# Moving the rotation of head 0's queries and keys behind sums of the second and third value group, on VectorE alone

## The chip, the cores and the metric

The kernel runs on one core of a Trainium2 chip. Its time is the device time of one execution in microseconds (us). A group of runs is given by its median. The engines are named as the profile names them: PE is TensorE (matmuls), PEld its weight loads, DVE is VectorE, ACT is ScalarE, POOL is GpSimd and SP is SyncE, which here only issues transfers.

## What is computed

The reference is a two-layer encoder in float32 over 512 tokens of width 1024. Layer 0 mixes tokens with a bidirectional mLSTM, layer 1 with attention in three dilation groups; after each mixer come a SwiGLU and a gated embedding. The change touches only the beginning of layer 1's mixer. There the normed input is projected to queries, keys and values of 8 heads for each of 3 groups, and a quarter of every query and key is rotated by position:

```python
def apply_partial_rope(x, cos, sin):
    half = ROPE_DIM // 2
    x1 = x[..., :half]
    x2 = x[..., half:ROPE_DIM]
    rot = jnp.concatenate([x1 * cos - x2 * sin, x2 * cos + x1 * sin], axis=-1).astype(x.dtype)
    return jnp.concatenate([rot, x[..., ROPE_DIM:]], axis=-1)
...
    proj = (xn @ w_in).reshape(B, S, N_GROUPS, 3, A_HEADS, A_HEAD_DIM)
    for g, (window, dil) in enumerate(DILATED_GROUPS):
        q = apply_partial_rope(proj[:, :, g, 0], cos, sin)
        k = apply_partial_rope(proj[:, :, g, 1], cos, sin)
        o_g, l_g = dilated_window_attention(q, k, proj[:, :, g, 2], dil, window // 2 // dil)
```

## The kernel before

Every large product is made of three float32r matmuls (L124 to L126): each operand is split into a rounded high part and the rest. Weights come from HBM into a ring of four staging tiles (`wst`); ACT rounds a piece to `wh` (L116), DVE subtracts to `wl` (L117), each in a ring of three; PE then multiplies.

Each engine runs its own queue strictly in order. The order in a queue is made when the program is built: a scheduler picks among what the code traces, and `tc.issue_after(ins)` ties whatever is traced inside it, on the engine of `ins`, to a place behind `ins`.

Layer 1's mixer begins like this:

- Six products make the queries and keys of head 0 for the three groups. They are made ahead, before the norm's factors are known, and ACT copies them out of PSUM into the tiles `ahead` (L1074).
- `value_cell(g)` makes the values of all heads for group g. It uses a seven-product scheme in place of eight quarter products: a11, s1, s2, s4, s3, a12, a22, in this order, each on quarters of the weights. One product is 2 halves (one `wh`/`wl` pair each) of 12 matmuls, so a group is 7 x 24 = 168 matmuls. Two of the seven weight operands are sums of two quarters, which POOL's queue makes by a second, accumulating transfer onto a landed quarter (L809); two others are made in place by DVE (L835, L838). Between the products DVE adds and subtracts the results (L850, L854, and the sums of outputs c12 at L859, c22 at L865, c21 at L875), and ACT evicts c11 (L870) and scales and stores the others (L831).
- `value_cell(0)` runs first. Then `qk_head(0, ahead)` rotates the six tiles of head 0, then `value_cell(1)` and `value_cell(2)` follow in the code, then `scores`.
- A rotation, `rope_evict`, is four instructions: DVE multiplies the tile by the cosines (L881) and shuffles 32 partitions (L883), POOL multiplies these by the sines (L884) and adds them in (L886). Group 0's query is then split into two parts by ACT and DVE (L951, L952); group 0's key is split into pieces by six copies on ACT (L941) and six subtractions on POOL (L942), with small fills (L944, L945). Where the tiles of group 0 are read, their tokens are reordered on the way, so operands are strided.

PSUM has three tiles of the kind `pj`, three of the kind `s` and two of the kind `o`. A value group takes three `pj`, one `s` and two `o`; its first and sixth product (a11, a12) use two `pj` tiles, which c11's eviction (L870) sets free for the next group.

Of the kernel before, what the change touches and what calls it, by code (L numbers as in the profile page):

```python
# [15 lines left out]
ALU = mybir.AluOpType  # L16
# [20 lines left out]
def encoder_kernel(  # L37
# [25 lines left out]
    V, A, G, T = nc.vector, nc.scalar, nc.gpsimd, nc.tensor  # L63
# [35 lines left out]
    def tok_a(t):  # L99
        return t.rearrange("p (u r) -> p u r", r=4)  # L100
# [48 lines left out]
    for hf in range(2):  # L149
        for i in range(4):  # L150
            if 4 * hf + i == 2:
                nc.sync.dma_start(nrow, norm_mix.rearrange("l (k p) -> (l k) p", p=P))
            t = ut()
# [130 lines left out]
    for hf in range(2):  # L284
        for i in range(4):
            t = ut()
# [398 lines left out]
    RS = cst.tile([32, S], F32, name="RS")  # L685
# [107 lines left out]

    vd = [dr.tile([S, D], F32, tag="vd", name=nm("vd"), bufs=3) for _ in range(3)]

    def value_cell(g):
        c0 = col(g, 2, 0)

        rows = vd[g].rearrange("(u r) c -> r u c", r=4) if g == 0 else vd[g].rearrange("(r u) c -> r u c", u=P)

        def part(e, c):
            return b_in[512 * e:512 * e + 512, c0 + 512 * c:c0 + 512 * c + 512].rearrange("(k p) c -> p k c", p=P)

        def quarter(e, c, plus=None):

            t = wp.tile([P, 4, 512], F32, tag="wst", name=nm("wst"), bufs=WST)
            nc.sync.dma_start(t, part(e, c))
            if plus:
                nc.gpsimd.dma_start(t, part(*plus), accum_op=ALU.add)  # L809
            return t  # L810

        def quad_product(o, name, w, prep=None, first=True):
            for e in range(2):
                d = w[:, 2 * e:2 * e + 2]
                if prep:
                    prep(d, slice(2 * e, 2 * e + 2))
                wh, wl = wsplit(d, (P, 2, 512))
                for t in range(2):
                    for kk in range(2):
                        xh, xl = n.quad(name, 2 * e + kk, t)  # L820
                        st = first and e == 0 and kk == 0
                        T.matmul(o[t], xh, wh[:, kk], start=st, stop=False, skip_group_check=True)
                        T.matmul(o[t], xh, wl[:, kk], start=False, stop=False, skip_group_check=True)  # L823
                        T.matmul(o[t], xl, wh[:, kk], start=False, stop=e == 1 and kk == 1,  # L824
                                 skip_group_check=True)

        def two():
            return [ut() for _ in range(2)]

        def store(t, half, c, src):  # L830
            A.activation(src, src, AF.Copy, scale=n.ra(2 * half + t))  # L831
            nc.sync.dma_start(rows[2 * half + t][:, 512 * c:512 * c + 512], src)

        def plus(b):
            return lambda d, ks: V.tensor_tensor(d, d, b[:, ks], op=ALU.add)  # L835

        def neg_plus(b):
            return lambda d, ks: V.scalar_tensor_tensor(d, d, -1.0, b[:, ks], op0=ALU.mult, op1=ALU.subtract)  # L838

        x_, z_, y_ = [ps(), ps()], [ps(), ps("s", (P, S), 3)], [ps("o", (P, S), 2) for _ in range(2)]  # L840
        b11, t1 = quarter(0, 0), quarter(0, 1, (0, 0))
        quad_product(x_, "a11", b11)
        m1 = two()
        for t in range(2):
            A.copy(m1[t], x_[t])
        b22 = quarter(1, 1)
        quad_product(z_, "s1", t1)
        w_ = two()
        for t in range(2):
            V.tensor_tensor(w_[t], z_[t], m1[t], op=ALU.subtract)  # L850
        quad_product(y_, "s2", t1, plus(b22))
        u2 = two()
        for t in range(2):
            V.tensor_tensor(u2[t], y_[t], m1[t], op=ALU.subtract)  # L854
        t3 = quarter(1, 1, (0, 1))
        quad_product(z_, "s4", b22, first=False)
        c12 = two()
        for t in range(2):
            V.tensor_tensor(c12[t], z_[t], u2[t], op=ALU.add)  # L859
            store(t, 0, 1, c12[t])  # L860
        b21 = quarter(1, 0)
        quad_product(y_, "s3", t3, first=False)
        c22 = two()
        for t in range(2):
            V.tensor_tensor(c22[t], y_[t], w_[t], op=ALU.add)  # L865
            store(t, 1, 1, c22[t])
        quad_product(x_, "a12", b21, first=False)
        c11 = two()
        for t in range(2):
            A.activation(c11[t], x_[t], AF.Copy, scale=n.ra(t))  # L870
            nc.sync.dma_start(rows[t][:, 0:512], c11[t])
        quad_product(y_, "a22", t1, neg_plus(b21), first=False)
        c21 = two()
        for t in range(2):
            V.tensor_tensor(c21[t], m1[t], y_[t], op=ALU.subtract)  # L875
            store(t, 1, 0, c21[t])

    def rope_evict(o, dst, b_layout):

        to = (lambda t: t) if b_layout else (lambda t: t.rearrange("p (r u) -> p u r", r=4))  # L880
        V.tensor_tensor(dst if b_layout else tok_a(dst), to(o), to(RC), op=ALU.mult)  # L881
        sh = ut((32, S))
        V.stream_shuffle(sh, o[0:32], [(e + 16) % 32 for e in range(32)])  # L883
        G.tensor_tensor(sh, sh, RS, op=ALU.mult)  # L884
        d = dst[0:32]
        G.tensor_tensor(d if b_layout else tok_a(d), d if b_layout else tok_a(d), to(sh), op=ALU.add)  # L886

    def values(pr):

# [20 lines left out]
    def product(g, s, h):  # L910

        c0 = col(g, s, h)
        stg = wp.tile([P, KT, 256], F32, tag="wst", name=nm("wst"), bufs=WST)
        nc.sync.dma_start(stg[:, :, :P], b_in[:, c0:c0 + P].rearrange("(k p) c -> p k c", p=P))
        wh, wl = wcols(stg, KT, 0)
        o = ps()
        for k in range(KT):
            mm3(o, wh[:, k], wl[:, k], n.xh[k], n.xl[k], k == 0, k == KT - 1)
        return o

    def qk_head(h, ahead=None):

        res = {}
        if ahead is None:
            ahead = {}
        for g in range(3):
            for s in range(2):
                o = ahead[g, s] if (g, s) in ahead else product(g, s, h)
                if g == 0 and s == 1:

                    t = ut()
                    rope_evict(o, t, False)
                    t4 = t.rearrange("p (i t) -> p i t", i=4)
                    kh, kl = ([ut((P, 2, 256), F32R) for _ in range(2)] for _ in range(2))

# [10 lines left out]
                    t = (kh, kl)  # L946
                elif g == 0:
                    t = ut()
                    rope_evict(o, t, False)
                    hi, lo = ut(dt=F32R), ut(dt=F32R)  # L950
                    A.copy(hi, t)  # L951
                    V.tensor_tensor(lo, t, f(hi), op=ALU.subtract)  # L952
                    t = (hi, lo)
                else:
                    t = ut()
                    rope_evict(o, t, True)
                res[g, s] = t
        return res

    def scores(qk):  # L960
        pA = [ut((P, 2, 256)) for _ in range(2)]
# [122 lines left out]
    V.tensor_tensor(RC[0:32], RC[0:32], rB[0:32], op=ALU.mult)  # L1084
    A.copy(RC[32:64], rB[32:64])
    A.copy(RC[64:P], rB[64:P])
    qk = qk_head(0, ahead)
    for g in range(1, 3):
        value_cell(g)
    probs = scores(qk)  # L1090
    for h in range(NH):
        if h % 2 == 0:
# [142 lines left out]
```

## Time and profile before

| | |
|---|---|
| Runs: median (lowest to highest of 3) | 1648.16 us (1646.62 to 1650.27) |
| The profiled execution's own time | 1647.76 us |
| Its span in the profile | 1646.1 us |
| DVE busy | 888.8 us (54%) |
| ACT busy | 629.1 us (38%) |
| POOL busy | 380.8 us (23%) |
| Transfers | 173.64 MB, 105 GB/s over the span |

A time in a row is counted from the start of the span. A row of the timeline gives the start, the duration, the engine, the line and the tiles, and in brackets how long the engine stood idle before it and what ended that. Matmuls overlap: with 512 columns one starts every 0.23 us, though each is shown longer. In a row of windows the columns are the length, each engine's busy time with the number of instructions, the granted TensorE clock as a share of full speed, the busy share of the DMA engines and GB/s. The three value groups lie between 731 and 866 us.

### The profile page before, as it was taken

Reading aid. Unit: us, or ns where it says so; the run is one execution under the profiler, and the core shown is the slowest. Engines: PE = TensorE matmul, PEld = TensorE weight load, DVE = VectorE, ACT = ScalarE, POOL = GpSimd, SP = SyncE. Lnnn points to the kernel's source line nnn. Section 1 sums busy time; section 2 is a strip of 40 time slices with the busy share of each in tenths; the row PEclk is TensorE's granted clock in tenths of the full one; section 3 lists DMA queues with packets and bytes.
Section 4 is the critical chain, followed back from the end, with each engine's and each line's share of the span. In section 5 each row is a group of like instructions: output and inputs, shape, how many; then the busy total and the mean of one; then the engine's idle time right before and its main releaser. Section 6 shows DMA issues by size and latency. Waiting matters only on the chain.

```text
span 1646.1 us, 20328 instructions
## 1 busy us (share of the span) xinstructions
PE 1601.9 (97%) x7892; PEld 1349.5 (82%) x7892; DVE 888.8 (54%) x1451; ACT 629.1 (38%) x1051; POOL 380.8 (23%) x459
## 2 busy tenths in 40 slices
PE   7899999999999999999899999999999999999998
PEld 6788998888888888787678788888788888888886
DVE  6755654444445333766867566666554444433353
ACT  5666543333232323654444233333343233223242
POOL 3455403000000010111604665656130000001000
PEclk9999999999999999999899999999999999999999
DMA  7322223223233322367466242425223323232221
GB/s 208 104 78 77 66 90 104 92 88 94 86 103 103 108 72 70 99 177 222 133 194 166 77 122 74 122 76 163 78 77 102 95 86 96 85 126 96 83 77 51
DMA packets 192496, 173.64 MB, mean 105 GB/s; under 512 B 16440, under 2 KB 171632, under 8 KB 192400
## 3 DMA queue, kind: packets, MB, share of 16 engines
q1 hardware_dynamic: 188096, 165.85, 32.7%
q0 software_dynamic: 3200, 6.36, 2.2%
q8 instruction: 62, 1.02, 0.3%
q10 hardware_dynamic: 1104, 0.13, 0.1%
q14 instruction: 34, 0.28, 0.1%
HBM read 163.85 MB, written 8.47 MB: 105 GB/s over the span
## 4 chain that ended last, share of the span: by engine, by line
PE 85%; DVE 3%; DMA 3%; POOL 2%; ACT 2%; issue 1%; POOLq 0%; SPq 0%; DVEq 0%; ACTq 0%
PE pj L124 19%; PE pj L125 19%; PE pj L126 19%; PE o L124 5%; PE o L126 5%; PE o L125 5%; PE o L498 2%; PE o L1031 2%; DMA wst<-in_b_w_in_dram 2%; DVE wl L117 1%; PE s L977 1%; ACT wh L116 1%; PE o L823 1%; PE o L824 1%; DMA swd<-st 1%
## 5 line engine op out<-in xcount | busy, mean ns | idle before, releaser
L116 ACT CAST wh<-wst 128x1024 fp32r<-128x1024 f32 (+2 forms) x285 | 289.5, 1020 | 653.7 <-PE pj L125 382.1
L124 PE MATMUL pj<-u,wh 128*128 128x512 f32 x1325 | 518.7, 391 | 2.7 <-ACT wh L116 1.5
L126 PE MATMUL pj<-u,wl 128*128 128x512 f32 x1325 | 517.6, 391 | 2.6 <-DVE wl L117 2.6
L125 PE MATMUL pj<-u,wh 128*128 128x512 f32 x1325 | 518.2, 391 | 0.0
L117 DVE TENSOR_TENSOR wl<-wst,wh 128x1024 fp32r<-128x1024 f32 (+3 forms) x283 | 341.6, 1208 | 212.8 <-ACT wh L116 212.4
L126 PEld LDWEIGHTS pj<-u,wl 128*128 128x128 f32 x1325 | 249.4, 188 | 55.5 <-DVE wl L117 4.4
L124 PEld LDWEIGHTS pj<-u,wh 128*128 128x128 f32 x1325 | 249.6, 188 | 54.8 <-ACT wh L116 2.2
L125 PEld LDWEIGHTS pj<-u,wh 128*128 128x128 f32 x1325 | 249.4, 188 | 50.5 <-DVE u L183 0.2
L241 POOL TENSOR_TENSOR u<-u,u 128x512 f32<-128x512 f32 x30 | 49.5, 1650 | 821.2 <-ACT u L237 820.9
L124 PE MATMUL o<-u,wh 128*128 128x512 f32 x375 | 146.1, 390 | 0.0
L126 PE MATMUL o<-u,wl 128*128 128x512 f32 x375 | 145.9, 389 | 0.0
L125 PE MATMUL o<-u,wh 128*128 128x512 f32 x375 | 145.9, 389 | 0.0
L884 POOL TENSOR_TENSOR u<-u,RS 32x512 f32<-32x512 f32 x48 | 90.4, 1883 | 127.7 <-DVE u L883 98.8
L613 DVE TENSOR_TENSOR u<-o,u 128x512 f32<-128x512 f32 x44 | 30.4, 691 | 127.5 <-PE o L126 123.7
L886 POOL TENSOR_TENSOR u<-u,u 32x512 f32<-32x512 f32 x48 | 82.3, 1715 | 3.8
L124 PE MATMUL pj<-wh,u 128*128 128x256 f32 (+1 forms) x272 | 79.3, 293 | 3.6 <-ACT u L432 3.6
L125 PEld LDWEIGHTS o<-u,wh 128*128 128x128 f32 x375 | 70.4, 188 | 14.6
L126 PEld LDWEIGHTS o<-u,wl 128*128 128x128 f32 x375 | 70.4, 188 | 14.6
L124 PEld LDWEIGHTS o<-u,wh 128*128 128x128 f32 x375 | 70.4, 188 | 14.5
L125 PE MATMUL pj<-wl,u 128*128 128x256 f32 (+1 forms) x272 | 79.5, 292 | 0.0
L126 PE MATMUL pj<-wh,u 128*128 128x256 f32 (+1 forms) x272 | 79.5, 292 | 0.0
L600 DVE TENSOR_TENSOR u<-pj,u 128x512 f32<-128x512 f32 x42 | 29.0, 691 | 81.9 <-PE pj L126 81.9
(316 smaller groups left out, 2056.1 us busy)
## 6 DMA issues: line engine op xcount, KB each, us to landing
wst<-in_b_w_in_dram SPq DMA_DIRECT2D x48, 512.0 KB, 3.8
wst<-in_w_gate_dram SPq DMA_DIRECT2D x22, 1024.0 KB, 5.3
wst<-in_w_up_dram SPq DMA_DIRECT2D x22, 1024.0 KB, 5.3
wst<-in_w_down_dram SPq DMA_DIRECT2D x16, 1024.0 KB, 5.2
wst<-in_b_w_in_dram SPq DMA_DIRECT2D x15, 1024.0 KB, 6.2
wst<-in_a_w_in_dram SPq DMA_DIRECT2D x8, 1024.0 KB, 5.3
wst<-in_ple_gate_dram SPq DMA_DIRECT2D x8, 1024.0 KB, 5.4
wst<-in_w_down_dram SPq DMA_DIRECT2D x8, 768.0 KB, 4.6
```

The source lines that it names most:

```text
L116: A.copy(hi, src)
L117: eng.tensor_tensor(lo, src, f(hi), op=ALU.subtract)
L124: T.matmul(o, ah, bh, start=start, stop=False)
L125: T.matmul(o, ah, bl, start=False, stop=False)
L126: T.matmul(o, al, bh, start=False, stop=stop_)
L241: (G if k < KT - 1 else V).tensor_tensor(self.q, self.q, s, op=ALU.add)
L498: T.matmul(o[:, d, :], pt[d][s][:, j * P:(j + 1) * P], vt[s][:, hh, :], start=s == ks[0], stop=s == ks[-1])
L600: V.tensor_tensor(gt, og_, n.rB, op=ALU.mult)
L613: V.tensor_tensor(u, ou, n.rB, op=ALU.mult)
L884: G.tensor_tensor(sh, sh, RS, op=ALU.mult)
L886: G.tensor_tensor(d if b_layout else tok_a(d), d if b_layout else tok_a(d), to(sh), op=ALU.add)
L1031: T.matmul(a_tile(o, i) if bi < 2 else b_tile(o, i), vv[i][:, e * P:(e + 1) * P], pt[:, i * P:(i + 1) * P], start=bi == 0 and i == 0, stop ...
```

## The change

`qk_head`'s body becomes a generator, `qk_steps`, that stops after each of the six query and key tiles. For head 0 the six steps are no longer traced between the first and the second value group: `value_cell(1)` and `value_cell(2)` each call one step behind the second half of c12, of c22 and of c21, inside `tc.issue_after` of that DVE instruction. So the order is query and key of group 0 and the query of group 1 in the second value group, then the key of group 1 and both of group 2 in the third. In these steps the two instructions that POOL did are done by DVE (`eng`); for heads 1 to 7 POOL keeps them.

```diff
@@ -793,7 +793,13 @@
-    def value_cell(g):
+    def value_cell(g, step=None):
+
+        def behind(ins):
+            if step:
+                with tc.issue_after(ins.ins):
+                    step()
+
...
@@ -856,14 +862,16 @@
         for t in range(2):
-            V.tensor_tensor(c12[t], z_[t], u2[t], op=ALU.add)
+            last = V.tensor_tensor(c12[t], z_[t], u2[t], op=ALU.add)
             store(t, 0, 1, c12[t])
+        behind(last)
         b21 = quarter(1, 0)
         quad_product(y_, "s3", t3, first=False)
         c22 = two()
         for t in range(2):
-            V.tensor_tensor(c22[t], y_[t], w_[t], op=ALU.add)
+            last = V.tensor_tensor(c22[t], y_[t], w_[t], op=ALU.add)
             store(t, 1, 1, c22[t])
+        behind(last)
...
         for t in range(2):
-            V.tensor_tensor(c21[t], m1[t], y_[t], op=ALU.subtract)
+            last = V.tensor_tensor(c21[t], m1[t], y_[t], op=ALU.subtract)
             store(t, 1, 0, c21[t])
-
-    def rope_evict(o, dst, b_layout):
+        behind(last)
+
+    def rope_evict(o, dst, b_layout, eng):
...
         V.stream_shuffle(sh, o[0:32], [(e + 16) % 32 for e in range(32)])
-        G.tensor_tensor(sh, sh, RS, op=ALU.mult)
+        eng.tensor_tensor(sh, sh, RS, op=ALU.mult)
         d = dst[0:32]
-        G.tensor_tensor(d if b_layout else tok_a(d), d if b_layout else tok_a(d), to(sh), op=ALU.add)
+        eng.tensor_tensor(d if b_layout else tok_a(d), d if b_layout else tok_a(d), to(sh), op=ALU.add)
...
-    def qk_head(h, ahead=None):
-
+    def qk_head(h):
         res = {}
-        if ahead is None:
-            ahead = {}
+        for _ in qk_steps(h, res):
+            pass
+        return res
+
+    def qk_steps(h, res, ahead=None):
+
+        eng = V if ahead else G
         for g in range(3):
             for s in range(2):
-                o = ahead[g, s] if (g, s) in ahead else product(g, s, h)
+                o = ahead[g, s] if ahead else product(g, s, h)
...
                 res[g, s] = t
-        return res
+                yield
...
-    qk = qk_head(0, ahead)
+    qk = {}
+    steps = qk_steps(0, qk, ahead)
     for g in range(1, 3):
-        value_cell(g)
+        value_cell(g, lambda: next(steps))
     probs = scores(qk)
```

In the changed kernel the lines that the text speaks of have other numbers: the rotation's four instructions L881, L883, L884, L886 are L890, L892, L893, L895 (all four on DVE for head 0); the in-place sums L835 and L838 are L841 and L844; L865, L870, L875, L941 are L872, L878, L883, L954; L850 and L859 are L856 and L865.

Three places in the queues matter below. Numbers in the names are buffers; `u_5854` and `u_5887` hold group 0's query and key of head 0.

DVE at the start of the second value group, before (first c21 of the first group, then rotations between the second group's weight pieces):

```order
L875 TENSOR_TENSOR u_6378<-u_6141,o_6102 128x512
L875 TENSOR_TENSOR u_6379<-u_6142,o_6103 128x512
L881 TENSOR_TENSOR u_6390<-u_5854,RC 128x512
L883 STREAM_SHUFFLE u_6392<-u_5854 32x512
L117 TENSOR_TENSOR wl_6500<-wst_6458,wh_6499 128x1024
L835 TENSOR_TENSOR wst_6458<-wst_6458,wst_6497 128x1024
L117 TENSOR_TENSOR wl_6516<-wst_6458,wh_6515 128x1024
L952 TENSOR_TENSOR u_6397<-u_6390,u_6396 128x512
L881 TENSOR_TENSOR u_6400<-u_5887,RC 128x512
L883 STREAM_SHUFFLE u_6402<-u_5887 32x512
L117 TENSOR_TENSOR wl_6537<-wst_6458,wh_6536 128x1024
```

DVE late in the second value group, now (from c12's second half to c22's second half; `wst_6566` and `wst_6398` are the weights of a12 and a22):

```order
L865 TENSOR_TENSOR u_6549<-s_6393,u_6510 128x512
L890 TENSOR_TENSOR u_6556<-u_5854,RC 128x512
L892 STREAM_SHUFFLE u_6558<-u_5854 32x512
L117 TENSOR_TENSOR wl_6635<-wst_6566,wh_6634 128x1024
L893 TENSOR_TENSOR u_6558<-u_6558,RS 32x512
L117 TENSOR_TENSOR wl_6651<-wst_6566,wh_6650 128x1024
L895 TENSOR_TENSOR u_6556<-u_6556,u_6558 32x512
L117 TENSOR_TENSOR wl_6674<-wst_6398,wh_6673 128x1024
L965 TENSOR_TENSOR u_6563<-u_6556,u_6562 128x512
L872 TENSOR_TENSOR u_6600<-o_6394,u_6471 128x512
L872 TENSOR_TENSOR u_6601<-o_6395,u_6472 128x512
```

The first rotation has moved from the start of the second group to behind c12, interleaved with the weight pieces of a12 and a22, and its last two steps have come over from POOL. The key's rotation follows in the same pattern behind c22, interleaved with a22's last piece and the third group's first.

DVE around the second group's third to fifth product (s2, s4, s3), before (`wst_6616` is the quarter b21, `wst_6497` and `wst_6573` the weights of s4 and s3):

```order
L117 TENSOR_TENSOR wl_6577<-wst_6497,wh_6576 128x1024
L854 TENSOR_TENSOR u_6569<-o_6454,u_6493 128x512
L854 TENSOR_TENSOR u_6570<-o_6455,u_6494 128x512
L117 TENSOR_TENSOR wl_6593<-wst_6497,wh_6592 128x1024
L117 TENSOR_TENSOR wl_6619<-wst_6573,wh_6618 128x1024
L838 SCALAR_TENSOR_TENSOR wst_6458<-wst_6458,wst_6616 128x1024
L859 TENSOR_TENSOR u_6608<-pj_6452,u_6569 128x512
```

DVE at the second group's third product (s2, pieces `wl_6477` and `wl_6494`), now (`wst_6566` is b21, `wst_6437` the weights of s4):

```order
L117 TENSOR_TENSOR wl_6477<-wst_6398,wh_6476 128x1024
L844 SCALAR_TENSOR_TENSOR wst_6398<-wst_6398,wst_6566 128x1024
L117 TENSOR_TENSOR wl_6494<-wst_6398,wh_6493 128x1024
L856 TENSOR_TENSOR u_6471<-pj_6392,u_6433 128x512
L856 TENSOR_TENSOR u_6472<-s_6393,u_6434 128x512
L844 SCALAR_TENSOR_TENSOR wst_6398<-wst_6398,wst_6566 128x1024
L117 TENSOR_TENSOR wl_6517<-wst_6437,wh_6516 128x1024
```

The subtraction that reads b21 (L838, now L844) has come forward from behind the first piece of s3 to between the two pieces of s2, and the second piece of s2 and the first of s4 now stand behind it.

ACT at the turn from the second to the third value group, before (`pj_6450` and `pj_6451` hold c11, `wst_6744` the third group's first weights):

```order
L831 ACTIVATE u_6650<-u_6650,rs_1031_5952 128x512
L831 ACTIVATE u_6651<-u_6651,rs_1031_5952 128x512
L116 CAST wh_6714<-wst_6458 128x1024
L870 ACTIVATE u_6690<-pj_6450,rs_1031_5952 128x512
L870 ACTIVATE u_6691<-pj_6451,rs_1031_5952 128x512
L116 CAST wh_6749<-wst_6744 128x1024
L116 CAST wh_6765<-wst_6744 128x1024
L116 CAST wh_6787<-wst_6746 128x1024
```

ACT at the same turn, now (`u_6608` is the rotated key of group 0; `pj_6390` and `pj_6391` hold c11):

```order
L116 CAST wh_6731<-wst_6726 128x1024
L116 CAST wh_6747<-wst_6726 128x1024
L954 CAST u_6614<-u_6608 128x2x128
L954 CAST u_6614<-u_6608 128x2x64
L954 CAST u_6615<-u_6608 128x2x128
L954 CAST u_6615<-u_6608 128x64
L954 CAST u_6614<-u_6608 128x64
L954 CAST u_6615<-u_6608 128x2x64
L878 ACTIVATE u_6666<-pj_6390,rs_1031_5952 128x512
L878 ACTIVATE u_6667<-pj_6391,rs_1031_5952 128x512
L116 CAST wh_6769<-wst_6728 128x1024
```

c11's two evictions have gone behind the third group's first two casts and behind the six copies of the key, which wait for its rotation on DVE.

## Rows read from the trace of the kernel before

**Rows 1.** The profile's page, section 1, busy time and share of the span.

```profile
PE 1601.9 (97%) x7892; PEld 1349.5 (82%) x7892; DVE 888.8 (54%) x1451; ACT 629.1 (38%) x1051; POOL 380.8 (23%) x459
```

**Rows 2.** Windows: the three value groups, then a piece of the second.

```profile
731.35:769.55 38.20, 38.20 (x172) 31.62 (x170) 28.55 (x30) 20.45 (x25) 1.28 (x1) 1.00 0.57 165
769.55:820.43 50.88, 43.43 (x170) 33.84 (x168) 43.36 (x48) 22.07 (x31) 31.91 (x24) 0.90 0.60 173
820.43:865.46 45.03, 41.45 (x169) 33.37 (x168) 27.78 (x29) 20.50 (x24) 1.90 (x3) 0.92 0.70 199
784.00:788.00 4.00, 4.00 (x11) 3.04 (x11) 4.00 (x5) 0.00 (x0) 3.92 (x2) 0.57 0.01 3
```

**Rows 3.** Timeline of PE: waits over 0.4 us inside the three groups, and one earlier.

```profile
700.94 0.50 PE L124 MATMUL pj<-u,wh 128*128 128x512 f32 x1 [1.24 <-ACT u L182]
...
781.38 0.50 PE L822 MATMUL o<-wh,u 128*128 128x512 f32 x1 [0.79 <-ACT wh L116]
783.96 0.50 PE L823 MATMUL o<-wl,u 128*128 128x512 f32 x1 [2.08 <-DVE wl L117]
...
790.60 0.73 PE L822 MATMUL o<-wh,u 128*128 128x512 f32 x2 [2.27 <-ACT wh L116]
793.53 0.80 PE L823 MATMUL o<-wl,u 128*128 128x512 f32 x1 [2.20 <-DVE wl L117]
...
829.14 0.79 PE L822 MATMUL pj<-wh,u 128*128 128x512 f32 x1 [3.11 <-ACT wh L116]
830.40 0.79 PE L823 MATMUL pj<-wl,u 128*128 128x512 f32 x1 [0.47 <-DVE wl L117]
```

**Rows 4.** Timeline of ACT in the second group.

```profile
779.76 0.62 ACT L951 CAST u<-u 128x512 fp32r<-128x512 f32 x1 [4.71 <-POOL u L886]
...
788.19 1.41 ACT L941 CAST u<-u 128x256 fp32r<-128x256 f32 x6 [6.86 <-POOL u L886]
```

**Rows 5.** Timeline of POOL in the second group.

```profile
775.51 1.27 POOL L809 DMA_DIRECT2D wst<-in_b_w_in_dram  x1 [15.61 <-DVE wst L835]
776.28 1.82 POOL L884 TENSOR_TENSOR u<-u,RS 32x512 f32<-32x512 f32 x1
```

**Rows 6.** Timeline of SP, one issue in the second group.

```profile
769.37 0.38 SPq L807 DMA_DIRECT2D wst<-in_b_w_in_dram  x1
```

**Rows 7.** DMA issues, windows 758:759, 813:814, 820:821 (last column: us to landing).

```profile
wst<-in_b_w_in_dram POOLq DMA_DIRECT2D x1, 1024.0 KB, 13.1
...
wst<-in_b_w_in_dram POOLq DMA_DIRECT2D x1, 1024.0 KB, 14.7
...
wst<-in_b_w_in_dram SPq DMA_DIRECT2D x1, 1024.0 KB, 12.8
```

**Rows 8.** Timeline of DVE in the first and second group.

```profile
758.43 1.28 DVE L865 TENSOR_TENSOR u<-o,u 128x512 f32<-128x512 f32 x2
...
770.45 1.30 DVE L881 TENSOR_TENSOR u<-u,RC 128x512 f32<-128x512 f32 x1
...
772.90 1.23 DVE L117 TENSOR_TENSOR wl<-wst,wh 128x1024 fp32r<-128x1024 f32 x1 [0.48 <-ACT wh L116]
...
784.97 1.78 DVE L881 TENSOR_TENSOR u<-u,RC 128x512 f32<-128x512 f32 x1
...
789.26 0.68 DVE L881 TENSOR_TENSOR u<-u,RC 128x512 f32<-128x512 f32 x1
...
794.61 1.79 DVE L117 TENSOR_TENSOR wl<-wst,wh 128x1024 fp32r<-128x1024 f32 x1
```

**Rows 9.** By line, 715:870 (last columns: busy us, mean ns of one, idle before).

```profile
L883 DVE STREAM_SHUFFLE u<-u 32x512 f32<-32x512 f32 x6 | 4.3, 718 | 0.0
L1084 DVE TENSOR_TENSOR RC<-RC,u 32x512 f32<-32x512 f32 x1 | 0.7, 671 | 0.0
L870 ACT ACTIVATE u<-pj,rs 128x512 f32<-128x512 f32 x6 | 4.0, 685 | 1.8 <-PE pj L824 1.8
L942 POOL TENSOR_TENSOR u<-u,u 128x256 fp32r<-128x256 f32 (+2 forms) x6 | 5.3, 902 | 0.4 <-ACT u L941 0.4
```

More of the change, by code (lines that the diff above doesn't have):

```diff
@@ L919, in product @@
         return o
-    def qk_head(h, ahead=None):
+    def qk_head(h):
         res = {}
-        if ahead is None:
-            ahead = {}
+        for _ in qk_steps(h, res):
[3 more added lines that the diff above has]
+        eng = V if ahead else G
         for g in range(3):
             for s in range(2):
-                o = ahead[g, s] if (g, s) in ahead else product(g, s, h)
+                o = ahead[g, s] if ahead else product(g, s, h)
                 if g == 0 and s == 1:
                     t = ut()
-                    rope_evict(o, t, False)
+                    rope_evict(o, t, False, eng)
                     t4 = t.rearrange("p (i t) -> p i t", i=4)
@@ L948, in qk_head @@
                     t = ut()
-                    rope_evict(o, t, False)
+                    rope_evict(o, t, False, eng)
                     hi, lo = ut(dt=F32R), ut(dt=F32R)
@@ L955, in qk_head @@
                     t = ut()
-                    rope_evict(o, t, True)
+                    rope_evict(o, t, True, eng)
                 res[g, s] = t
-        return res
+                yield
     def scores(qk):
```

## The prediction

> **What bounds the kernel now.** The page comes first: PE is busy for 97% of the span [rows 1], so VectorE (DVE), ScalarE (ACT), GpSimd (POOL) and the transfers cost time only where PE waits for them. The windows say where that is. The three value groups do the same 168 matmuls each. The first takes 38.20 us, the second 50.88, the third 45.03 [rows 2]. The first shows what a group costs when nothing is late: 38.20 / 168 = 0.227 us a matmul, 2.73 a half product, 5.46 a product. Against it the second group loses 12.68 us and the third 6.83, together 19.5. That is all there is to win here.
>
> PE's timeline says how the 12.68 are lost. Four waits of 0.79, 2.08, 2.27 and 2.20 us [rows 3] make 7.34. The other 5.3 is speed: from 784 to 788 us the granted clock is 0.57 of full, near the lower of its two levels (1.2 and 2.4 GHz), and only 11 matmuls start where 17 would [rows 2]. In the third group two waits of 3.11 and 0.47 us make 3.58 [rows 3], so 3.25 is slow clock. A lone wait of 1.24 us earlier in the run [rows 3] has no slow stretch behind it.
>
> ACT and POOL show the cause. The waits end when ACT or DVE delivers a weight piece. ACT was late because it stood 4.71 us and then 6.86 us behind POOL's L886, the last step of a rotation [rows 4]. POOL could not start the first rotation at once: in its queue an accumulating transfer stands ahead, which was issued only at 775.51 after 15.61 us, and L884 follows at 776.28 [rows 5]. DVE meanwhile is slowed by POOL's work: a weight piece takes 1.79 us at 794.61 instead of 1.23 [rows 8]. So the second group's loss is the rotation's. The third group's loss is its heir, as I read it: the weight piece that PE waits 3.11 us for comes from an accumulated quarter that lands 14.7 us after issue [rows 7], and it could be issued only when a late DVE had set a staging tile free.
>
> **The change, part by part.** *Removed:* in these two groups POOL's 12 rotation instructions, the waits of ACT on them, the slowed DVE, and 6 rotations from the start of the second group. All 19.5 us are open: -19.5.
>
> *Added on DVE:* 12 instructions of 32x512. Nearest row: a 32x512 product on DVE takes 0.67 us [rows 9]. With the multiply (0.68 dense [rows 8]) and the shuffle (0.72 [rows 9]) a rotation of group 1 or 2 is 0.68 + 0.72 + 2 x 0.67 = 2.74 us of DVE. For group 0 the operands are strided. The multiply then took 1.30 without POOL beside it and at most 1.78 for any of the six [rows 8]; I take 1.25. The strided add has no row. It lies between 0.67 and 1.30, and I take 1.0, since only one of its inputs jumps. A first-group DVE load of 28.55 us in 38.20 [rows 2] leaves 9.6 free, so DVE can carry it, but not without queues. The times below count products of 5.46 us from the second group's start at 769.55. Four places pay.
>
> *(a) s2 and s4 of the second group.* The subtraction that reads b21 now stands in front of the second piece of s2. Without other stops s2 runs from 780.5 to 785.9 and its second piece is due at 783.4. b21's load was issued at 769.37 [rows 6]. Its own landing is not shown. The same load took 12.8 us in the third group [rows 7], which gives 782.2; transfers were over by 784 (busy share 0.01 from there [rows 2]). So: subtract to 783.4, split to 784.6, stop 1.2. Then two differences (1.28 [rows 8]), a second subtraction and a split, 1.23 each, to 788.4, where s4 is due at 787.3: stop 1.1. Together **2.3**. Ends: 0 if b21 lands by 781, 4.1 if at 784.
>
> *(b) The start of the third group.* Its first product writes the two PSUM tiles that hold c11. Their evictions now wait for the six key copies, and these for the key's rotation. From c12 (ready at about 791.0 without stops) DVE has: two sums and a query rotation's first two steps 1.28 + 1.25 + 0.72; splits and steps 1.23 + 0.67 + 1.23 + 1.0 + 1.23; the query's low part, as long as a dense pass, 0.68; two sums 1.28; the key's 1.25 + 0.72; 1.23 + 0.67 + 1.23 + 1.0. Sum 16.7, to 807.7. Copies 1.41 [rows 4] and the first eviction 0.69 [rows 9] give 809.8. PE wants that tile 6 matmuls after 807.75, at 809.1. Stop **0.7**; with dense prices 0, with the contended multiply twice and adds of 1.30, 2.4.
>
> *(c) s1 and s2 of the third group.* The group 1 query's rotation stands among the splits of s1, and the two in-place sums for s2 behind it. Beside POOL's six key subtractions (5.3 us [rows 9]) a split takes about 1.75. After a split (1.23) and c21 (1.28) DVE is at 810.2: multiply and shuffle to 811.6, split 813.3, step 0.97 beside POOL, split 816.0, add 816.7, two sums 819.2, split 820.4. Due at 819.6, as (b) has moved it. Stop **0.8**. Ends: 0 with POOL out of the way; 2.4 if the accumulated quarter takes 14.7 us instead of the 13.1 of the second group [rows 7] and adds its 1.6. Beside POOL's ops the trace stretches a split from 1.23 to 1.79 and not further [rows 8]. The Trainium skill, "SBUF — State Buffer", section "Who interferes with whom", has it that a DVE instruction with two SBUF inputs and a GpSimd one that reads SBUF lock each other out for the whole instruction. By the row (c) is 0.8; by the rule it is up to 4.8, a rival below.
>
> *(d) Scores.* The last rotation comes after c21 and ahead of the scores it feeds; scores and PSUM tiles wait on it. Seven DVE steps of about 0.7 against matmuls of head 1 that were put between leave **0.6**, between 0 and 1.3.
>
> The third group's stop on its transfer (3.11) goes, because the splits that free its staging tiles run on time again; the second group's same transfer, at 13.1 us, stopped nothing. The rotations issue no transfers. In POOL's queue that accumulating transfer now stands ahead of all rotation work, and the next one behind the six subtractions, which end long before its first half has landed. In SP's queue only one load moves: its tile is freed by a22's last split, some 2 us later than in the first group, and it is needed a whole half group after. Heads 1 to 7 keep their instructions.
>
> **Sum.** -19.5 + 2.3 + 0.7 + 0.8 + 0.6 = -15.1 us. On the profiled execution's 1647.76 that is 1632.7. The median of the runs shown, 1648.16, is 0.4 above it, so 1633.1, in round numbers **1633.0 us**. The ends of the four places add to 0 and 10.2: 1628.7 to 1638.9.
>
> **The rivals.**
> - *The slow clock comes back briefly* in one or both groups, because a stop of 1.2 us and one of 1.1 come 4 us apart. For it: in the second group 0.79 and 2.08 together were enough [rows 3]. Against it: the lone 1.24 was not. Price 5.3 and 3.25, as above: 1636 to 1641.5. Chance 0.15.
> - *POOL's subtractions hold DVE off* for their whole 5.3 us instead of stretching it by 1.3 as counted: place (c) becomes 0.8 + 4.0 = 4.8, time 1637. The row of 1.79 speaks against it. Chance 0.05.
> - *The third group's transfer stays late*, at 14.7 us or more, since other loads still go beside it: only the second group's 12.68 comes back, less (a), (b), (d): 1648.2 - 12.68 + 3.6 = 1639. Chance 0.09.
> - *Transfers are the bound* of groups two and three: 7 loads of 1 MB and 8 stores of 0.25 MB, 9.4 MB, at the third group's 199 GB/s [rows 2] take 47.4 us, two groups 94.8 against 95.9 now: about 1647, no change. Against it: a busy share of 0.01 from 784 to 788 [rows 2] is room, all loads in flight had landed by then, and the first group's matmuls ran through in 38.20. Chance 0.06.
> - *Slower: the lower clock stays.* Place: from s2 of the second group on, where each of (a), (b), (c) stops PE shortly. At the lower level a matmul takes twice 0.227. The 15.1 us are used up after 67 slow matmuls, under three products. If all 108 from s2's second half to that group's end ran slow, 24.5 us go: 1657.5. Against it: at half speed DVE has twice the time, so the stops end themselves, and after 3.58 us of waits the old third group lost only 3.25 to the clock. Chance 0.06. The Trainium skill, "TensorE: Matmul & The Clock Gate", section "A second HAM failure mode: psum-queue depth-cycling", tells of a kernel whose frequent short idles moved the clock between its levels; no run here shows that from stops this short.
>
> That the change doesn't do what it says is excluded by the order: all 12 instructions stand on DVE, each step behind its sum.
>
> **How the numbers follow.** The forecast has 0.58, the rivals 0.41, and 0.01 is for what I don't see, put to no change. Faster by over 0.2% (3.3 us, about what a measurement of this kernel can tell): 0.58 + 0.15 + 0.05 + 0.09 = 0.87. Same: 0.06 + 0.01 = 0.07. Slower: 0.06. The range is 1629 to 1641: the forecast's own ends, the brief slow clock nearly whole, the held-off DVE and the late transfer; it leaves out the last two rivals and a rest, some 0.16.
>
> **What would show it.** Right: ACT no longer waits on POOL in these groups, the second group takes 40 to 42 us and the third 39 to 42, the clock near 1.00 in both, and PE waits of about 1 us at s2, s4, the third group's first product and its s2. Wrong: a group over 45 us; a clock under 0.9; a wait of 3 us on an accumulated quarter; or PE waiting over 2 us at the scores.

## The result and the profile after

The changed kernel takes 1626.21 us (1624.62 to 1628.91, 4 runs). The kernel before, beside it, takes 1649.12 us (1646.62 to 1650.27, 4 runs). The ratio is 0.9865, with a 95% interval of 0.9844 to 0.9885. Two later measurements gave 1623.62 against 1644.83 and 1624.0 against 1644.81. So the change saves 21 to 23 us, where 15.1 were forecast, and the measured time lies below the range.

The three value groups, which answer to [rows 2], are now alike (columns as there):

```profile
729.36:767.56 38.20, 38.20 (x172) 31.62 (x170) 28.55 (x30) 20.39 (x25) 1.28 (x1) 1.00 0.60 172
767.56:805.70 38.14, 38.14 (x170) 31.59 (x169) 33.92 (x39) 20.69 (x27) 3.25 (x5) 1.00 0.88 246
805.70:843.90 38.20, 38.20 (x171) 31.64 (x170) 35.04 (x45) 22.33 (x29) 6.89 (x11) 1.00 0.72 220
```

The second and the third take what the first takes, at a granted clock of 1.00. PE's list of waits is empty from 715 to 950 us: nothing stands where [rows 3] has the waits of the groups, and none of the four forecast stops came. DVE carries 5.4 to 6.5 us more than in the first group, in time in which it stands idle there.

ACT at the turn to the third group, against [rows 4]: it waits 0.55 us, on DVE and not on POOL.

```profile
804.77 1.41 ACT L954 CAST u<-u 128x256 fp32r<-128x256 f32 x6 [0.55 <-DVE u L895]
806.09 1.26 ACT L878 ACTIVATE u<-pj,rs 128x512 f32<-128x512 f32 x2
```

POOL, against [rows 5]: a group has two accumulating transfers. The third group's first is issued at 794.96, ahead of the key's subtractions, and lands after 12.3 us; its second is issued right behind them.

```profile
807.04 3.69 POOL L955 TENSOR_TENSOR u<-u,u 128x256 fp32r<-128x256 f32 x4
810.68 1.29 POOL L815 DMA_DIRECT2D wst<-in_b_w_in_dram  x1
```

DVE, against [rows 8]: the subtraction of b21, the first strided multiply and add, and the pieces beside POOL's subtractions.

```profile
776.39 1.22 DVE L117 TENSOR_TENSOR wl<-wst,wh 128x1024 fp32r<-128x1024 f32 x1
777.65 1.23 DVE L844 SCALAR_TENSOR_TENSOR wst<-wst,wst 128x1024 f32<-128x1024 f32 x1
...
789.02 0.68 DVE L865 TENSOR_TENSOR u<-pj,u 128x512 f32<-128x512 f32 x1
...
790.22 1.30 DVE L890 TENSOR_TENSOR u<-u,RC 128x512 f32<-128x512 f32 x1
...
803.66 1.08 DVE L895 TENSOR_TENSOR u<-u,u 32x512 f32<-32x512 f32 x1
...
808.46 1.22 DVE L117 TENSOR_TENSOR wl<-wst,wh 128x1024 fp32r<-128x1024 f32 x1
809.60 0.80 DVE L893 TENSOR_TENSOR u<-u,RS 32x512 f32<-32x512 f32 x1
810.63 1.23 DVE L117 TENSOR_TENSOR wl<-wst,wh 128x1024 fp32r<-128x1024 f32 x1 [0.23 <-ACT wh L116]
```

There is a second place that changed, and the prediction did not look there: the scores of head 1. In the kernel before PE waited for POOL's last rotation step; in the changed kernel it does not. PE of the kernel before:

```profile
912.63 1.83 PE L977 MATMUL s<-u,u 128*128 128x128 f32 x14 [2.80 <-POOL u L886]
```

**The account.** From the first value matmul to the last the kernel before took 133.88 us and the changed one takes 114.13: 19.75 of the 23.1 us between the two profiled executions. Of the rest, 1.99 us lie ahead of the groups, where the program is the same: in the profiles of this study the groups begin anywhere from 728.9 to 733.2 us. Behind the groups only 1.4 us were gained (780.8 against 779.4; 776.0 and 776.6 in two later profiles of the change). So the stop of 2.80 at head 1 is gone from the timeline, but what it was worth is not measured: by the medians, 1.1 to 3.2 us of the gain lie outside the groups.

### The profile page after: what moved, and what is told of

Read it like the earlier page. It is cut to its first block, busy times and chain, and to the rows that moved or that the text cites. A ratio compares the mean times of both kernels' runs of the same rounds, so it can differ in the third digit from the quotient of the medians.

```text
span 1622.9 us, 20315 instructions
## 1 busy us (share of the span) xinstructions
PE 1591.7 (98%) x7892; PEld 1344.0 (83%) x7892; DVE 887.8 (55%) x1463; ACT 628.1 (39%) x1051; POOL 356.2 (22%) x447
## 4 chain that ended last, share of the span: by engine, by line
PE 90%; ACT 3%; DVE 2%; POOL 2%; DMA 1%; issue 1%; SPq 0%; POOLq 0%; DVEq 0%; ACTq 0%
PE pj L124 20%; PE pj L125 20%; PE pj L126 20%; PE o L124 5%; PE o L126 5%; PE o L125 5%; PE o L498 2%; PE o L1044 2%; POOL u L478 1%; PE pj L830 1%; PE o L830 1%; PE o L829 1%; PE pj L829 1%; PE pj L828 1%; PE o L828 1%
## 5 line engine op out<-in xcount | busy, mean ns | idle before, releaser
L893 POOL TENSOR_TENSOR u<-u,RS 32x512 f32<-32x512 f32 x42 | 76.1, 1812 | 117.8 <-DVE u L892 95.2
L600 DVE TENSOR_TENSOR u<-pj,u 128x512 f32<-128x512 f32 x42 | 29.0, 691 | 81.6 <-PE pj L126 81.6
L895 POOL TENSOR_TENSOR u<-u,u 32x512 f32<-32x512 f32 x42 | 72.5, 1727 | 3.3
```

The source lines that it names most:

```text
L893: eng.tensor_tensor(sh, sh, RS, op=ALU.mult)
L895: eng.tensor_tensor(d if b_layout else tok_a(d), d if b_layout else tok_a(d), to(sh), op=ALU.add)
```

## The experiments

In this table "groups" is the time from the start of the first of the 504 value matmuls to the start of the last, in the profiled execution. Times are medians in us, and "before" is the kernel before, measured beside the run. "And" stands for the change with something added.

| run | what it is | groups | time | before |
|---|---|---|---|---|
| before | | 133.9 | | |
| e2_engine_only | old place, all on DVE | 130.8 | 1643.28 | 1646.14 |
| e11_old_fills | old place, POOL's two steps read nothing | 127.4 | 1636.52 | 1645.45 |
| e1_place_only | new place, POOL's two steps stay | 121.0 | 1634.37 | 1646.14 |
| e3_no_tail | old place, multiply alone | 117.7 | 1628.85 | 1646.14 |
| r_after, r_after2 | the change | 114.2, 114.2 | 1623.62, 1624.0 | 1644.83, 1644.81 |
| e4_all_dve | and heads 1 to 7 on DVE | 114.2 | 1623.81 | 1646.14 |
| e5_head1_late, e9_head1_later | and head 1's key later | 114.2, 114.2 | 1624.26, 1624.61 | 1644.83, 1644.81 |
| e7_key_late | and 2.6 us of DVE ahead of the key | 116.3 | 1626.66 | 1644.83 |
| e10_pool_fill | and POOL filling tiles | 116.1 | 1625.12 | 1644.81 |
| e6_pool_beside | and POOL multiplying tiles | 124.1 | 1638.39 | 1644.83 |

**The change is two things, a place and an engine.** The first two runs make one without the other.

```diff
-        eng = V if ahead else G
+        eng = G
```

> The steps stand where the change puts them, but POOL still does the two sine steps of head 0's rotations. Theory A (the loss was the rotation's last steps in POOL's queue, behind an accumulating transfer that waits, with ACT and so PE behind them): the transfer of the third group's a-quarter still stands in that queue, so ACT waits on POOL again at the key's copies and PE stops at the turn to the third group; the two groups lose 5 us or more, time 1631 to 1640. Theory B (the loss was six rotations bunched at the second group's start; the engine does not matter): both groups at 38.2 to 39 us, time 1626 to 1628. For head 1's stop of 2.8 us at its scores (C: it hangs on whether the key's rotation of head 1 stands on DVE ahead of head 0's normalisation): it stands ahead here, so the stop is gone.

The place alone brings 12.9 of the groups' 19.75 us (ratio 0.9925, 0.9908 to 0.9941). A's bounds hold: the groups lose 6.8 us against the change, the time lies between 1631 and 1640, and PE stops at the turn to the third group. B's do not. But A as a whole account fails, since most of the old loss is gone while POOL still has its two steps. Head 1's stop is gone. PE's longer waits in the groups and at head 0's scores:

```profile
805.88 0.50 PE L829 MATMUL o<-wl,u 128*128 128x512 f32 x1 [1.92 <-DVE wl L117]
814.55 0.50 PE L829 MATMUL pj<-wl,u 128*128 128x512 f32 x1 [0.76 <-DVE wl L117]
823.72 0.50 PE L829 MATMUL pj<-wl,u 128*128 128x512 f32 x1 [0.70 <-DVE wl L117]
859.94 1.42 PE L990 MATMUL s<-u,u 128*128 128x128 f32 x10 [2.27 <-POOL u L895]
```

The three in the groups end with DVE's weight pieces. Behind the first two stands ACT, which waits on POOL's last rotation step again, and DVE's pieces come after ACT's copies:

```profile
800.33 0.62 ACT L964 CAST u<-u 128x512 fp32r<-128x512 f32 x1 [3.61 <-POOL u L895]
...
809.73 1.41 ACT L954 CAST u<-u 128x256 fp32r<-128x256 f32 x6 [5.14 <-POOL u L895]
```

This time no transfer stands ahead of POOL's steps: the key's waited on DVE's shuffle and then took 3.29 and 1.53 us. The third wait is DVE's own: beside POOL's next two steps (818.19 to 822.6) a sum and a piece of 1.23 us take almost double.

```profile
819.23 2.21 DVE L841 TENSOR_TENSOR wst<-wst,wst 128x1024 f32<-128x1024 f32 x1
821.36 2.31 DVE L117 TENSOR_TENSOR wl<-wst,wh 128x1024 fp32r<-128x1024 f32 x1
```

The engine alone, in the old place (`eng` passed to the kernel before):

```diff
+        eng = V if ahead else G
...
-        G.tensor_tensor(sh, sh, RS, op=ALU.mult)
+        eng.tensor_tensor(sh, sh, RS, op=ALU.mult)
```

> The old place (all six rotations of head 0 ahead of the second group), but all four instructions on DVE. Theory A: without POOL nothing waits behind a transfer; the DVE load of 6 rotations of 2.7 to 3.7 us at the second group's start costs a few stops, the group takes 39 to 43 us and the third 38.2 to 39, time 1628 to 1634. Theory B: the bunch is still there and has 12 instructions more, the second group stays at 48 us or more, time 1642 to 1650. C: the key's rotation of head 1 stands behind head 0's normalisation as before, so PE stops 2.8 us at head 1's scores again.

It brings only 3.1 us (0.9979, 0.9970 to 0.9989). PE's two longest waits in the groups:

```profile
787.26 0.50 PE L823 MATMUL o<-wl,u 128*128 128x512 f32 x1 [1.94 <-DVE wl L117]
...
798.11 0.80 PE L822 MATMUL pj<-wh,u 128*128 128x512 f32 x1 [6.82 <-DVE u L850]
```

DVE's queue is the cause. From the third rotation's multiply it runs rotations alone for 10.3 us, while the difference L850 that PE waits for stands behind them:

```profile
787.14 1.21 DVE L881 TENSOR_TENSOR u<-u,RC 128x512 f32<-128x512 f32 x1
...
796.79 0.67 DVE L884 TENSOR_TENSOR u<-u,RS 32x512 f32<-32x512 f32 x1
797.39 0.67 DVE L850 TENSOR_TENSOR u<-pj,u 128x512 f32<-128x512 f32 x1
```

So B holds for this half, with 54.7 us for the second group: the bunch is a cause of its own. Head 1's stop is there, with 1.66 us and not 2.8. The halves alone bring 12.9 and 3.1, both together 19.75.

**How much was POOL?** First the rotation's tail was left out:

```diff
+        if eng is V:
+            return
         sh = ut((32, S))
```

> The old place, and head 0's rotation is cut to its first instruction: the shuffle, the product with the sines and the sum are left out for head 0. This is what the groups cost with no tail of the rotation at all. Theory A: 38.2 to 39 us in each group, about the time of the change plus head 1's stop, 1627 to 1630. Theory B: six products of 0.7 to 1.3 us still bunched, the second group 39 to 42. C: head 1's stop of 2.8 us stays, since the order there is as before.

Six bunched multiplies alone cost 3.6 us against the change (117.7 against 114.1), with stops of 1.18 and 0.51 us: more than the 1.6 that A allows, and inside B's bounds, though the time is in A's. So of the old 19.75 us some 16 came with the tail. Head 1's stop was there with 1.12 us, not 2.8. The last run of the study took the tail apart. It changes what POOL's two steps read, and nothing else: DVE's and ACT's order is that of the kernel before.

```diff
+        if fill:
+            for _ in range(2):
+                G.memset(sh, 0.0)
+            for _ in range(2):
+                G.memset(d, 0.0)
+            return
         G.tensor_tensor(sh, sh, RS, op=ALU.mult)
```

> The kernel before, its place, its order on DVE and ACT and the place in POOL's queue all unchanged; only the two instructions of head 0's rotations on POOL, which read two tiles each, become two fills each of 32x512, which read none (the product with the sines and the sum are left out for head 0). K (POOL and DVE holding each other off at SBUF is the larger part of the old loss): DVE's seven lengthened instructions of the second group (4.9 us over their plain times) go back to 1.23, ACT still waits on POOL behind the accumulating transfer but for less, and the two groups lose 3 to 9 us in place of 19.5: time 1628 to 1634. L (the bunch and the place in POOL's queue are the larger part): they lose 13 us or more: 1638 to 1645.

The groups still lose 13.3 us, so it is L by a little; the time lies between the two forecasts, and at most 6.4 us are K's. In the kernel before DVE had rows like these beside POOL's steps:

```profile
802.18 2.30 DVE L838 SCALAR_TENSOR_TENSOR wst<-wst,wst 128x1024 f32<-128x1024 f32 x1
...
805.01 1.71 DVE L117 TENSOR_TENSOR wl<-wst,wh 128x1024 fp32r<-128x1024 f32 x1
```

With fills the same instruction is back at its plain time, and none in the two groups is lengthened by over 0.2 us:

```profile
797.81 1.22 DVE L838 SCALAR_TENSOR_TENSOR wst<-wst,wst 128x1024 f32<-128x1024 f32 x1
```

ACT still waits behind POOL's queue, for the query's copy 3.7 us where it had been 4.71 and for the key's 2.1 where it had been 6.86 [rows 4]:

```profile
ACT u L957 <- POOL u L889: 3.7, 1, 3.7
ACT u L947 <- POOL u L889: 2.1, 1, 2.1
```

A fill is shorter than what it replaces (two take 1.1 us), so the 6.4 us hold POOL's shorter work too, and this run does not part the two.

The next run goes the other way: the changed kernel gets POOL work that nobody waits for, four products of 32x512 behind each rotation.

```diff
+                if ahead:
+                    r = t if g else rot[0]
+                    spare = ut((32, S))
+                    for _ in range(4):
+                        G.tensor_tensor(spare, r[0:32], RS, op=ALU.mult)
```

> The change, and POOL gets four products of 32x512 behind each of head 0's six rotations, 24 in all, about 30 us of POOL work that nobody waits for. E (POOL's work stretches DVE's and so cost the groups before): weight pieces of 1.23 us take up to 1.8 us beside it, DVE loses 5 to 10 us over two groups, PE stops 2 to 5 us: time 2 to 8 us over the change's. F (the stretch is rare and DVE has room): a few pieces are stretched, PE does not stop, within 0.5 us of the change.

It costs 14.8 us, nearly twice the upper end of E. PE's waits:

```profile
812.06 0.80 PE L828 MATMUL pj<-wh,u 128*128 128x512 f32 x1 [2.65 <-ACT u L878]
...
835.03 0.50 PE L829 MATMUL pj<-wl,u 128*128 128x512 f32 x1 [3.27 <-DVE wl L117]
...
863.50 0.58 PE L124 MATMUL s<-u,u 128*128 128x256 f32 x1 [2.53 <-DVE mx L993]
```

The clock falls with them (0.74 from 836 to 842 us), which E had not counted. DVE is held off, here in an instruction of 1.23 us that stands in its queue ahead of the piece PE waits 3.27 us for:

```profile
826.67 3.88 DVE L844 SCALAR_TENSOR_TENSOR wst<-wst,wst 128x1024 f32<-128x1024 f32 x1
```

The second accumulating transfer, behind POOL's products in its queue, is late too. It is issued 94.3 us after the first value matmul, where the change's profiles have 81.3 (after), 87.0 (r_after) and 81.6 (r_after2), and ACT waits for it:

```profile
834.07 1.99 ACT L116 CAST wh<-wst 128x1024 fp32r<-128x1024 f32 x2 [6.88 <-DMA wst<-in_b_w_in_dram]
```

But these casts are for s3, and PE's wait of 3.27 is in the product before it, s4; s3 then began without a wait. So none of the three waits of PE ends with the transfer, though it might have cost something had DVE been on time. To part the two, three of each four products became six fills:

```diff
-                    for _ in range(4):
-                        G.tensor_tensor(spare, r[0:32], RS, op=ALU.mult)
+                    G.tensor_tensor(spare[0:32], r[0:32], RS, op=ALU.mult)
+                    for _ in range(6):
+                        G.memset(spare, 0.0)
```

> The run with POOL's 24 added products, but 18 of them are fills of a 128x512 tile with zeros (36 fills in place of 18 products), which read nothing; one product stays behind each rotation so that all still wait for it. The place in POOL's queue is the same. G (POOL and DVE get in each other's way at SBUF when both read): DVE's instructions take their plain 1.23 and 0.67 us, the fills are short, the accumulating transfer of the third group is issued within 1 us of the change's place, PE does not stop: the change's time within 1 us. H (it is POOL's queue: the transfer stands behind POOL's work, and DVE's long instructions are only a side effect): the transfer is 4 us late or more, and PE stops 2 to 3 us on it again: 4 us or more over the change's.

The time is 1.1 us over r_after2's, near G and far from H. The transfer is late as H had it, 88.7 us after the first value matmul, 7.1 later than in r_after2 beside it, but PE does not stop on it: a delay of that size has room. PE has one small stop, elsewhere:

```profile
809.55 0.50 PE L828 MATMUL pj<-wh,u 128*128 128x512 f32 x1 [0.60 <-ACT u L878]
```

A fill takes 0.54 us, two of them less than the 1.25 to 2.3 of a product, so the queue was emptier as well, and a delay as long as e6's stays untested. Beside one of the products that were left DVE again took 2.31 us for 1.22. The Trainium skill, "SBUF — State Buffer", section "Who interferes with whom", says that a VectorE instruction with two SBUF inputs contends with a GpSimd one that reads SBUF, not with one that only writes it. These runs agree: 3.88 us beside products, 1.22 beside fills.

**How much room place (b) has.** Two more strided multiplies ahead of the key's rotation:

```diff
+                    if ahead:
+                        for _ in range(2):
+                            V.tensor_tensor(tok_a(t), o.rearrange("p (r u) -> p u r", r=4),
+                                            RC.rearrange("p (r u) -> p u r", r=4), op=ALU.mult)
                     rope_evict(o, t, False, eng)
```

> The change, and DVE makes the strided product of the key's rotation three times in place of once, 2.6 us more in front of the key's copies. Place (b) of the prediction was right in kind and had room by a hair (the change's trace: the first eviction of c11 ends about 0.3 us before PE wants the tile): PE stops 2.0 to 2.6 us at the third group's first product, time 2 to 3 us over the change's (up to 5 if the clock falls with it). Rival (DVE has idle time in that stretch that takes it up): stop under 1 us, within 1 us of the change.

The time rises by 3.0 us as expected and the groups by 2.1, but the stop is shorter than the 2.0 to 2.6 us expected, and at another place: not at c11's eviction, but half a product earlier, where a22's last weight piece now stands behind the added multiplies.

```profile
807.72 0.50 PE L829 MATMUL o<-wl,u 128*128 128x512 f32 x1 [1.52 <-DVE wl L117]
```

So this stretch takes up about 1 us and no more, although DVE is idle for over 4 us of the second group: idle time elsewhere in a group is no room here.

**Head 1's stop.** In the kernel before the rotation of head 1's key stood on DVE behind the normalisation of head 0; in the changed one the scheduler puts it ahead. It was put back by half, behind the minimum `mn`:

```diff
-        V.tensor_tensor(mn, so[:, :, 0], ng[:, 1], op=ALU.min)
+        mns.append(V.tensor_tensor(mn, so[:, :, 0], ng[:, 1], op=ALU.min))
...
+                    if h == 1:
+                        with tc.issue_after(mns[0].ins):
+                            rope_evict(o, t, False, eng)
```

> The change, but the rotation of head 1's key is queued on DVE behind the normalisation of head 0 (the minimum mn), as the kernel before had it. C (head 1's stop comes from this place in DVE's queue alone): PE stops 1.5 to 3 us at head 1's scores, time 1.5 to 3 us over the change's. Rival (that stop was the heir of head 0's late rotations, by POOL still being behind): no stop, time as the change's within 0.5 us.

No stop, time 0.6 us over r_after's: C was wrong as it stood. But the multiply began 0.1 us after `mn`, not 2.1 us as in the kernel before. Put behind the product with `dB`, DVE's order around it is that of the kernel before:

```diff
-        V.tensor_tensor(dn[:, 1], e2[:, 1], dB, op=ALU.mult)
+        dns.append(V.tensor_tensor(dn[:, 1], e2[:, 1], dB, op=ALU.mult))
```

> The change, with the rotation of head 1's key queued still later on DVE, behind the products of head 0's normalisation, about where the kernel before had it (there its multiply began 2.1 us after the minimum mn, in the last experiment on this 0.1 us after). C, as corrected (POOL's chain of head 1, 22 us from the key's first sine step to its last sum, had 1.7 us of room in the change, so it depends on how late this place is): the chain starts about 2.5 us later than there, PE stops 0.5 to 2.5 us at head 1's scores, time 0.5 to 2.5 us over the change's. Rival (the chain's own length, 23.0 us in the kernel before against 21 to 24 us in the others, is what made the stop there, not the place): no stop, time as the change's within 0.5 us.

The stop is back in PE's timeline, in the slowest of the four executions:

```profile
893.45 1.83 PE L996 MATMUL s<-u,u 128*128 128x128 f32 x14 [1.45 <-POOL u L895]
```

Its POOL rows are the key's first sine step and the last sum of the head:

```profile
869.40 1.28 POOL L893 TENSOR_TENSOR u<-u,RS 32x512 f32<-32x512 f32 x1 [7.95 <-DVE dn L1019]
...
892.15 1.25 POOL L895 TENSOR_TENSOR u<-u,u 32x512 f32<-32x512 f32 x1
```

and in r_after:

```profile
862.62 2.16 POOL L893 TENSOR_TENSOR u<-u,RS 32x512 f32<-32x512 f32 x1 [3.33 <-DVE u L892]
...
887.06 1.29 POOL L895 TENSOR_TENSOR u<-u,u 32x512 f32<-32x512 f32 x1
```

Counted from the start of the last value matmul (847.33 and 845.17), PE wants the last sum after 44.7 us. In e9 POOL ends after 46.1, in r_after after 43.2, in the kernel before it was 47.3. The other profiles bear the place out. Counted from the same point, the key's multiply began at 19.48, 19.95, 20.14, 20.19 and 21.15 us in e3, e11, e2, e9 and the kernel before, and PE stopped 1.12, 1.49, 1.66, 1.45 and 2.80 us: about the later, the longer. At 19.04 (e5) and at 15.64 (r_after) it did not stop. What the stop is worth in time is not settled: e9's median is 0.6 us over r_after2's, and its runs go from 1623.82 to 1629.71.

**Repeats, and one step further.** The change itself, run again twice beside the others:

> The change itself once more, beside the next three. By theory D (its gain is the groups' 19.7 us and head 1's 2.8 us, nothing else) it stands 22 to 23 us under before; if part of the first measurement was a lucky draw of the stretch ahead of the groups, 20 to 21 us.

> The change itself, beside the other two, for their comparison: 21 to 23 us under before.

It saved 21.2 us (0.9874, 0.9852 to 0.9896) and 20.8 us (0.9871, 0.9856 to 0.9886). That is under the 22 to 23 of D and nearer to the 20 to 21 that stood for a lucky stretch ahead of the groups in the first measurement, whose 22.9 lies in the same intervals. Last, the sine steps of heads 1 to 7 were moved to DVE too:

```diff
-        eng = V if ahead else G
+        eng = V
```

> The change, and in addition the sine steps of heads 1 to 7 on DVE too. If POOL's queue and the stretching of DVE beside POOL cost something in the heads, 0.5 to 3 us are gained (1623 to 1626). If DVE is the later of the two there, the 84 added instructions of 0.67 us show as stops at the scores: 1627 to 1635. No difference (1626 plus or minus 1) if all of it has room.

1623.81 us, ratio 0.9863 (0.9848 to 0.9877): as the change. So the 84 instructions that POOL does for heads 1 to 7 cost nothing that shows here, and no version beats the change.

## Why the prediction was wrong

The direction and the main mechanism were right: the groups' losses were the rotation's, and the third group's stop on its transfer went with them. Two steps failed, both to the same side.

- *"Sum. -19.5 + 2.3 + 0.7 + 0.8 + 0.6."* The 19.5 measured 19.75. The four stops, 4.4 us, measured 0. That alone gives 1628.7, the sum's own lower end, and 1626.21 was measured.
  - (a) took the landing of b21's load from the third group's row of 12.8 us [rows 7]. Here the load was issued at 767.38, and L844 began at 777.65, straight behind the piece before it: it had landed within 10.3 us. Why the two loads differ is not shown. The lower end, 0, held.
  - (b) was right in kind and mis-sized by about 1 us. From c12's first sum (789.02) to the key's last add (804.74) it is 15.7 us, not 16.7: each instruction starts some 0.08 us before the end that is shown for the one ahead of it, and the sum added shown durations. PE wanted the tile at 807.00, and the first eviction ended some 0.2 us before. The strided add, taken as 1.0, is 1.08.
  - (c) began 1 us late by (b)'s error and let POOL's six subtractions stretch a split to 1.75 us. The two splits took 1.22 and 1.23, and one 32x512 product 0.80 for 0.67. In r_after a split took 1.59, and PE did not stop there either.
  - (d) DVE's last rotation steps fitted between the scores' maxima.
- *"That is all there is to win here."* PE stood 2.80 us at head 1's scores, outside the stretch that was summed; how much of the gain this made is open. "Heads 1 to 7 keep their instructions" was true of their number and said nothing of their order, which the scheduler changed. The order of both kernels showed it; it was read at three places only.

*"Beside POOL's ops the trace stretches a split from 1.23 to 1.79 and not further"* was wrong too, though it did not move the sum much. In the kernel before itself a split took 2.31 us (at 799.95) and a sum 2.30, and e6 had 3.88. The rival that POOL holds DVE off describes a real mechanism, up to 6.4 us of the old loss. It cost nothing in the change, where only six subtractions were left to meet DVE. "Which end long before its first half has landed", of these six, failed as well: in r_after2 the transfer waited 0.57 us for that landing, and in r_after the subtractions themselves held the transfer back. It had room in each.

And the cause was put on POOL's queue and POOL's slowing of DVE; the bunch on DVE was not priced. Taken off one by one, the 19.75 us are 3.6 for six bunched multiplies, 9.7 more for the tail behind the transfer and in the bunch, and 6.4 for POOL's steps reading beside DVE and being longer than fills. In another order the shares would differ: with all on DVE, the bunch alone cost 16.6. The brief slow clock, the late transfer, the transfers' bound and the lasting slow clock did not show.

## What to carry to other kernels

Where a stage beside the change runs through at full speed with the same matmuls, take its length as what the changed stages can reach. Charge forecast stops against it only where a landing or a queue was measured in the stage itself: the stops here, each of 0.6 to 1.2 us and worked out from shown durations and borrowed landings, came to nothing. When a scheduler sets the order, compare the order beyond the edited stretch, and look there for waits that could go or come. To move work off a late place, try place and engine apart: here the place alone left a third of the loss and the engine alone five sixths.

## What was not expected of the hardware

- Products on POOL (GpSimd) that read two tiles hold DVE instructions with two SBUF inputs off: 1.23 us became up to 3.88 us. Sums with one PSUM input kept 0.68 us beside them, and fills on POOL, which read nothing, left the others at 1.22.
- It is not every instruction. In r_after three pieces lie wholly beside POOL's subtractions and took 1.21 to 1.59 us, while POOL's own 32x512 steps, 1.25 us alone, took up to 3.3 us beside DVE (e1): the delay falls now on the one, now on the other. The four subtractions that take 3.69 us in the rows of POOL above took 8.14 in r_after, the same program, and the transfer behind them was issued later:

```profile
809.87 8.14 POOL L955 TENSOR_TENSOR u<-u,u 128x256 fp32r<-128x256 f32 x4
817.95 1.30 POOL L815 DMA_DIRECT2D wst<-in_b_w_in_dram  x1
```

- Work on POOL that nobody waits for cost 14.8 us (e6), through three waits of PE (2.65, 3.27, 2.53) and a clock of 0.74 after the second of them.
- The length of a stop alone did not decide on the clock. A stop of 1.52 us (e7) left the granted clock at 1.00; one of 1.92 (e1) was followed by 0.59 for 4 us; the 2.80 at head 1 in the kernel before was followed by 1.00.
